# First loads in another order, a last stage on two queues and two engines, in a two-layer decoder trunk

## The chip, the cores and the metric

The kernel runs on one core of a Trainium2 chip. A core has a matrix engine (TensorE, PE in the profile), a vector engine (VectorE, DVE), an engine for functions of one argument (ScalarE, ACT), a general engine (GpSimd, POOL) and one that mostly issues transfers (SyncE, SP). Transfers between the chip's main memory and the core's own memory are issued into queues; an engine that issues one does so in its own order of instructions. The metric is the time of one execution on the device, in microseconds (us); smaller is better. "Profiled execution" is one further run that the hardware profiler recorded.

## The reference

Input is one sequence of 256 tokens with 1024 features and one conditioning vector c. The trunk has two layers; each is a half-step feed-forward block (FFN), a token mixer (stick-breaking attention in layer 0, a gated linear recurrence in layer 1), and another half-step FFN. Ahead of every block x is normalised and shifted and scaled by vectors that are made from c:

```
c_act = silu(c)
mod   = (c_act @ mod_w[layer] + mod_b[layer]).reshape(B, 3, 3, D)    # per block: shift, scale, gate
h     = rmsnorm(x, norm_g) * (1 + scale) + shift
x     = x + weight * (1 + gate) * block(h)                            # weight 0.5 for an FFN, 1 for a mixer
swiglu(h) = (silu(h @ w_g) * (h @ w_u)) @ w_down
...
out   = rmsnorm(x, final_norm_g)
```

All of it is in float32. Some 250 MB of weights are read once.

## The kernel before

x is kept transposed: 8 chunks of 128 features by 256 tokens, in one tile `xall`. Weights come as raw tiles of 1 MB, in a ring of three (`raw`). ScalarE rounds each to a high part (`wh`, L516) and VectorE makes the low part as the difference (`wl`, L519); TensorE adds three products per block of weights (high by high, high by low, low by high; L545).

The shift, scale and gate vectors are made by VectorE. `mod_tile` (L570 to L579) loads 512 KB of `modw` into a ring of three (`rawm`), and one instruction (L577) multiplies it by silu(c), which stands in all 128 partitions (`cact`), and adds up along the row. There are 144 such tiles. `mod_final` adds the bias and finishes a vector. `hook` (L1219) hands out these tiles between the weight tiles of each block.

All loads go through SP's one queue, in program order. The program is first recorded as a list of operations, and a planner (`Program.schedule`) then writes a fixed order for each engine: it simulates the list with a cost for each operation (`c_dma`, `c_act`, `c_dve`, `c_mm`) and takes the operation with the earliest due time among those that could start. So an edit of an early operation or of its cost can move instructions anywhere in the program, not only at the place of the edit. A load's cost is its bytes by 360 a ns plus 20 ns; the first loads wait for one another by `chained` with a latency of 950 ns (`LAT0`).

Between two blocks the work goes so. `down` (L663) finishes the 8 chunks of a block's output; `residual` (L686) adds each to x on VectorE; `add_square` (L603 to L614) squares it on ScalarE and adds the squares up on VectorE (`ssq`); `scaled` (L629 to L639) makes from it the next block's input without its norm (`hx`), in two parts. `rstd` (L616) lets TensorE sum the squares over partitions with a matrix of ones (L621), and ScalarE makes the reciprocal root (`rst`). TensorE meanwhile begins the next block on the input without norm (`up_first`, L734), and `norm_chunk` (L642 to L649) makes the input with norm. Modulation products and weight splits stand between all these on VectorE, in the order that the planner wrote.

The first block has no block before it. `first_loads` (L1175) loads x in four pieces of two chunks, c behind the first of them, and squares the chunks on ScalarE and, for chunks 1 and 7, on VectorE; TensorE spreads c over the partitions and ScalarE makes silu of it. The first scale and shift tiles, the first part of the parameters (`pars`, biases and norm weights) and the first weights (`gu0`) follow.

The last stage, `final` (L1157), multiplies x by `rst` on VectorE (L1162) in six pieces of 1, 1, 2, 2, 1 and 1 chunks, and SP stores each (L1164).

Of the kernel before, what the change touches and what calls it, by code (L numbers as in the profile page):

```python
# [10 lines left out]
AF = mybir.ActivationFunctionType  # L11
# [19 lines left out]
HALF = 1024  # L31
SQ = 8
NFIRST = 2
LAT0 = 950.0
SMALL = (0, 7)
HXPAD, HKPAD, ARPAD = 112, 16, 64
KICKS = (2, 3, 7, 9, 11, 15, 19)
# [321 lines left out]
    return (432.0 if passes == 4 else 114.0 * passes) * max(n, 256) / 256  # L359


def c_dma(n):
    return n * P * 4 / 360.0 + 20.0


@with_exitstack
def trunk(ctx, tc, xT, cb, par, modw, gu0, gu, wdn, qk, wv, wo, win, wri, wout, out):
# [74 lines left out]
    def fixed(name, cols, dt=F32):  # L442
        return const.tile([P, cols], dt, tag=name, name=name)
# [35 lines left out]
    def col(off, n=1):  # L479
        return pars()[:, off : off + n]  # L480
# [6 lines left out]
    fixed("pad1", ARPAD)  # L487


    def dma(dst, src, n, w, after=(), lat=None):  # L490
        return pr.op("DMA", c_dma(n), lambda: sp.dma_start(dst(), src), w=w, after=after, lat=lat)

    def A(o, i, f, n, r, w, table=None, psum=False, ptr=0, after=(), **kw):
        def fn():
            act.activation(o(), i(), f, **{k: (v() if callable(v) else v) for k, v in kw.items()})  # L495
        return pr.op("ACT", c_act(n, psum, ptr), fn, r, w, after, table)

    def V(fn, n, r, w, cost=None, ptr=0):
        return pr.op("DVE", cost or c_dve(n) + 62.0 * ptr, fn, r, w)
# [67 lines left out]
        return acc.group(part, o, w, wc, xs, xc, stop, parts)  # L567


    def mod_tile(l, s, w, t, after=(), lat=None):  # L570

        m = mraw[l, s, w]
        raw = Buf(modr)
        load_ = dma(raw, modw[l, (s * 3 + w) * KD + t], D, [raw], after, lat)

        def fn():
            dve.scalar_tensor_tensor(raw(), raw(), 1.0, cact(), ALU.mult, ALU.mult, accum_out=m()[:, t : t + 1])  # L577
        V(fn, D, [raw, cact], [raw, (m, t)])
        return load_  # L579

    def mod_final(l, s, w, t0=0, n=KD):
        m, f = mraw[l, s, w], mfin[l, s, w]
        b = OFF_MB + (l * 9 + s * 3 + w) * KD + t0
        rr = [(m, t) for t in range(t0, t0 + n)]
        ww = [(f, t) for t in range(t0, t0 + n)]
        pp = [(pars, 0)] if l == s == 0 else [pars]
        mi = lambda: m()[:, t0 : t0 + n]
        fo = lambda: f()[:, t0 : t0 + n]
        if w == 0:
            V(lambda: dve.tensor_tensor(fo(), mi(), col(b, n), ALU.add), n, rr + pp, ww)  # L590
            return
        V(lambda: dve.tensor_tensor(mi(), mi(), col(b, n), ALU.add), n, rr + pp, rr)
        if w == 1:
            g = OFF_NG + (l * 3 + s) * KD + t0
            V(lambda: dve.scalar_tensor_tensor(fo(), mi(), 1.0, col(g, n), ALU.add, ALU.mult), n, rr + pp, ww)
        else:
            wt = MAC if s != 1 else 1.0
            V(lambda: dve.tensor_scalar(fo(), mi(), 1.0, wt, ALU.add, ALU.mult), n, rr, ww)
# [172 lines left out]
    def ffn(l, s, nxt, hook):  # L771
        j = 2 * l + (s == 2)
        R, F = new_phase(2 * NF * 2, 0)
        ys = []

        def tile_out():
            ys.append((Buf(R, 2), Buf(R, 2)))
            return ys[-1]

        if j == 0:  # L780
            f0 = SQ
            accs = [Acc(f"g0_{f}") for f in range(SQ)]
            q = rstd((0, 0))

            def early(k, w):
                if k < KD:
                    last[:] = [mod_tile(0, 0, w, k, last, LAT0)]
                    if k == 0 and w == 0:
                        chained(lambda: pars()[:, :NP0], par[:, :NP0], NP0, [(pars, 0)])
                        mod_final(0, 0, 1, k, 1)  # L790
                    if k or w == 0:
                        mod_final(0, 0, w, k, 1)

            early(0, 1)
            early(0, 0)
            dma(lambda: pars()[:, NP0:], par[:, NP0:], NPAR - NP0, [(pars, 1)])
            for k in range(KD):
                norm_chunk((0, 0), k, q)
                size = HALF // 2 if k in SMALL else HALF
                done = [0]  # L800

                def chain(dst, src, n, w):
                    chained(dst, src, n, w)
                    done[0] += n
                    if done[0] % HALF == 0:
                        early(k + 1, 2 - done[0] // HALF)

                ws = load(gu0[k], CH, f"gu0_{k}", chain, size)
                for f in range(SQ):
                    for g in range(2):  # L810
                        i, c0 = divmod((f * 2 + g) * P, size)
                        group(accs[f], (g, 0), lambda b, g=g: b[:, g * T : (g + 1) * T], ws[i],
                              lambda u, c0=c0: u[:, c0 : c0 + P], hcur[0, 0][k], lambda v: v[:, :T], T, k == KD - 1)
            for f in range(SQ):
                swiglu_tile(accs[f], tile_out())
            other_copy((0, 0))
        else:
            f0 = NFIRST

            def first_out(g, gr, gc, u, ur, uc):  # L820
                sg, a = Buf(sgr), Buf(ar)
                A(sg, g, AF.Silu, T, [g, gr], [sg], table="silu", ptr=1, bias=gc)
                V(lambda: dve.scalar_tensor_tensor(a(), u(), uc(), sg(), ALU.add, ALU.mult), T, [u, ur, sg], [a], ptr=1)
                split(tile_out(), a, T)

            for (g, gr, gc), (u, ur, uc) in up_first((l, s), [load(gu[j, f], CH, f"gu_{j}_{f}") for f in range(f0)]):
                first_out(g, gr, gc, u, ur, uc)
        for f in range(f0, NF):
            hook(f)
            acc = Acc(f"g_{j}_{f}")  # L830
            up(acc, load(gu[j, f], CH, f"gu_{j}_{f}", chained if j == 0 and f == f0 else None), (l, s), f in KICKS)
            swiglu_tile(acc, tile_out())
        down(l, s, nxt, [wdn[j, :, 2 * c : 2 * c + 2, :].rearrange("p k d -> p (k d)") for c in range(NF // 2)],
             lambda k: (ys[k], slice(0, T)), 2, lambda c: hook(NF + 2 * c))
# [322 lines left out]
    def final():  # L1157
        q = rstd("end")

        def put(d0, n):  # L1160
            o = xall[:, d0 * T : (d0 + n) * T].rearrange("p (d t) -> p d t", d=n)
            V(lambda: dve.tensor_tensor(o, o, q().unsqueeze(1).to_broadcast([P, n, T]), ALU.mult), n * T,  # L1162
              x[d0 : d0 + n] + [q], x[d0 : d0 + n])
            pr.op("DMA", c_dma(n * T), lambda: sp.dma_start(out[:, d0 : d0 + n, :], o), x[d0 : d0 + n], [])  # L1164

        for d0, n in ((0, 1), (1, 1), (2, 2), (4, 2), (6, 1), (7, 1)):
            put(d0, n)


    last = []  # L1170

    def chained(dst, src, n, w):
        last[:] = [dma(dst, src, n, w, last, LAT0)]

    def first_loads():  # L1175
        c, b = Buf(modr), [Buf(banks), Buf(banks)]

        total = Buf(ssqr)

        def square(d):  # L1180
            p, q = [total if d + i == 0 else Buf(sqr if i else hpr) for i in range(2)]
            A(p, x[d], AF.Square, T, [x[d]], [p])
            if d in (0, KD - 2):
                V(lambda: dve.tensor_tensor(q(), x[d + 1](), x[d + 1](), ALU.mult), T, [x[d + 1]], [q])
            else:
                A(q, x[d + 1], AF.Square, T, [x[d + 1]], [q])

            def add(a, b):
                V(lambda: dve.tensor_tensor(a(), a(), b(), ALU.add), T, [a, b], [a])

            if d == KD - 2:
                add(p, q)
                ssq[0, 0] = (total, p)
            else:
                if d:
                    add(total, p)
                add(total, q)

        for d in range(0, KD, 2):
            o = xall[:, d * T : (d + 2) * T].rearrange("p (d t) -> p d t", d=2)  # L1200
            chained(lambda o=o: o, xT[:, d : d + 2, :], 2 * T, x[d : d + 2])
            if d == 0:
                last[:] = [pr.op("DMA", 450.0, lambda: sp.dma_start(c()[:1, :], cb), [], [c], last, lat=LAT0 - 440.0)]
                for h in range(2):
                    cs = slice(h * 512, (h + 1) * 512)
                    pr.op("PE", 4 * 427.0, lambda h=h, cs=cs: pe.matmul(b[h]()[:, :], ones[:1, :], c()[:1, cs], start=True,
                                                                        stop=True), [c], [b[h]])
                    A(lambda cs=cs: cact()[:, cs], b[h], AF.Silu, 512, [b[h]], [(cact, h)], table="silu", psum=True)
            square(d)

    first_loads()

# [92 lines left out]
```

## Time and profile before

| what | us |
|---|---|
| median of three runs | 964.43 |
| the three runs | 965.01, 964.43, 962.86 |
| the profiled execution | 971.47 |
| its span, which the rows below count from 0 | 969.8 |
| TensorE busy in the span | 950.1 |
| VectorE busy | 796.6 |
| ScalarE busy | 563.3 |
| GpSimd busy | 2.3 |

The mean granted clock of TensorE in the profiled execution was 0.996 of full speed. A row of a timeline reads: start, duration, engine, line of the kernel and operation, what is written from what is read, number of instructions taken together, and in brackets how long the engine stood idle before it and what ended that. A row of a group reads: line, engine, operation, count, then busy time and mean duration in ns, then idle time before. A row of stages reads: stretch, its length, busy time (and instructions) of TensorE, its weight loads, VectorE, ScalarE and GpSimd, the granted clock, the busy share of the transfer engines, and GB/s.

### The profile page before, as it was taken

The page shows a single profiled execution, that of the slowest core. Times are in us where ns is not written, and L with a number is a line of the kernel's source. Part 1 is how long each engine was busy: PE and PEld are TensorE (multiplying, and loading weights), DVE is VectorE, ACT ScalarE, POOL GpSimd, SP SyncE. Part 2 cuts the span into 40 slices and gives each one's busy share as a digit, 9 for nine tenths or more (in the row PEclk, how much of TensorE's full clock was granted, in tenths as well). Part 3 has the DMA queues.
Part 4 walks back from the last instruction along what each step waited for, and adds up shares of the span by engine and source line. Part 5 has one row for each costly group of instructions (what it writes and reads, how often), then busy time and mean ns, then how long its engine had stood idle before and what let it go on. Part 6 is the DMA issues. An engine that isn't in the chain of part 4 may idle for free.

```text
span 969.8 us, 19744 instructions
## 1 busy us (share of the span) xinstructions
PE 950.1 (98%) x8102; PEld 937.1 (97%) x8102; DVE 796.6 (82%) x1322; ACT 563.3 (58%) x908; POOL 2.3 (0%) x15
## 2 busy tenths in 40 slices
PE   6999999999999999999999999999999999999996
PEld 4999999999999999999989999999999999999996
DVE  7998888798998999889789999854997997555443
ACT  5475444388886854454356544443879785454343
POOL 0000000000000000000000000000000000000000
PEclk9999999999999999999999999999999999999999
DMA  8989999945766399999976999975334646555531
GB/s 315 369 308 357 323 355 353 344 190 188 252 216 207 139 362 334 338 352 363 345 255 237 339 366 355 345 276 189 116 137 168 261 142 250 199 193 192 172 116 44
DMA packets 48332, 251.25 MB, mean 259 GB/s; under 512 B 5489, under 2 KB 6129, under 8 KB 28530
## 3 DMA queue, kind: packets, MB, share of 16 engines
q1 hardware_dynamic: 48242, 249.99, 70.6%
q8 instruction: 63, 1.03, 0.4%
q14 instruction: 27, 0.22, 0.1%
HBM read 248.92 MB, written 1.05 MB: 258 GB/s over the span
## 4 chain that ended last, share of the span: by engine, by line
PE 71%; DVE 12%; DMA 10%; ACT 3%; issue 2%; SPq 1%; DVEq 0%
PE bank L545 65%; DMA rawm<-in_modw 10%; DVE wl L519 4%; DVE rawm L577 3%; PE bank L866 2%; DVE arenaf L1045 1%; PE bank L989 1%; ACT wh L516 1%; ACT arenaf L495 1%; DMA raw<-in_gu 1%; PE bank L562 1%; PE bank L942 1%; DVE x L686 1%; DVE hx L649 1%; PE bank L967 1%
## 5 line engine op out<-in xcount | busy, mean ns | idle before, releaser
L545 PE MATMUL bank<-hx,wh 128*128 128x256 f32 (+1 forms) x3236 | 564.8, 279 | 3.9 <-ACT hx L495 3.1
L545 PEld LDWEIGHTS bank<-hx,wh 128*128 128x128 f32 x3236 | 493.7, 189 | 6.6 <-ACT hx L495 3.9
L516 ACT ACTIVATE wh<-raw 128x1024 fp32r<-128x1024 f32 (+1 forms) x328 | 336.7, 1046 | 273.1 <-PE bank L545 192.6
L519 DVE TENSOR_TENSOR wl<-raw,wh 128x1024 fp32r<-128x1024 f32 (+1 forms) x328 | 388.7, 1207 | 97.2 <-ACT wh L516 96.2
L545 PE MATMUL bank<-hx,wl 128*128 128x256 f32 (+1 forms) x1618 | 449.8, 278 | 0.0
L545 PEld LDWEIGHTS bank<-hx,wl 128*128 128x128 f32 x1618 | 306.1, 189 | 0.0
L545 PE MATMUL bank<-arenar,wh 128*128 128x256 f32 x1664 | 285.0, 277 | 0.0
L545 PEld LDWEIGHTS bank<-arenar,wh 128*128 128x128 f32 x1664 | 250.8, 188 | 0.1
L545 PE MATMUL bank<-arenar,wl 128*128 128x256 f32 x832 | 229.7, 276 | 0.0
L577 DVE SCALAR_TENSOR_TENSOR rawm<-rawm,cact 128x1024 f32<-128x1024 f32 x144 | 174.8, 1220 | 31.6 <-DMA rawm<-in_modw 31.1
L545 PEld LDWEIGHTS bank<-arenar,wl 128*128 128x128 f32 x832 | 156.2, 188 | 0.0
L495 ACT ACTIVATE arenar<-a 128x256 fp32r<-128x256 f32 x88 | 35.5, 406 | 23.2 <-DVE a L764 18.9
L769 DVE TENSOR_TENSOR arenar<-a,arenar 128x256 fp32r<-128x256 f32 x88 | 36.3, 418 | 1.0 <-ACT arenar L495 1.0
L495 ACT ACTIVATE sg<-bank 128x256 f32<-128x256 f32 x82 | 30.0, 367 | 8.9 <-PE bank L545 8.8
L764 DVE TENSOR_TENSOR a<-bank,sg 128x256 f32<-128x256 f32 x82 | 34.0, 417 | 1.5 <-ACT sg L495 1.1
L495 ACT ACTIVATE hx<-hpre,mf 128x256 fp32r<-128x256 f32 x48 | 23.4, 500 | 17.3 <-DVE mf L590 12.3
L495 ACT ACTIVATE hx<-x,mf 128x256 fp32r<-128x256 f32 x40 | 18.8, 502 | 22.3 <-DVE x L686 22.3
L545 PE MATMUL bank<-hk,wh 128*128 128x256 f32 x156 | 31.0, 290 | 0.0
L686 DVE SCALAR_TENSOR_TENSOR x<-bank,mf,x 128x256 f32<-128x256 f32 x48 | 21.7, 477 | 7.8 <-PE bank L545 7.7
L545 PEld LDWEIGHTS bank<-hk,wh 128*128 128x128 f32 x156 | 24.0, 188 | 0.5
L649 DVE SCALAR_TENSOR_TENSOR hx<-hpre,mf,hx 128x256 fp32r<-128x256 f32 x48 | 22.9, 480 | 1.8 <-ACT hx L495 1.8
L866 PE MATMUL bank<-wh,hx 128*128 128x256 f32 x128 | 23.4, 281 | 0.4 <-DVE hx L649 0.4
(106 smaller groups left out, 537.7 us busy)
## 6 DMA issues: line engine op xcount, KB each, us to landing
raw<-in_gu SPq DMA_DIRECT2D x79, 1024.0 KB, 5.6
rawm<-in_modw SPq DMA_DIRECT2D x144, 512.0 KB, 6.7
raw<-in_wdn SPq DMA_DIRECT2D x44, 1024.0 KB, 6.9
raw<-in_win SPq DMA_DIRECT2D x10, 1024.0 KB, 4.8
raw<-in_qk SPq DMA_DIRECT2D x8, 1024.0 KB, 5.5
raw<-in_gu SPq DMA_DIRECT2D x14, 512.0 KB, 5.7
raw<-in_wout SPq DMA_DIRECT2D x5, 1024.0 KB, 5.3
raw<-in_wv SPq DMA_DIRECT2D x4, 1024.0 KB, 4.9
```

The lines of the kernel that those rows point to most:

```text
L495: act.activation(o(), i(), f, **{k: (v() if callable(v) else v) for k, v in kw.items()})
L516: act.activation(h()[:, :m], raw()[:, a : a + m], AF.Copy)
L519: dve.tensor_tensor(lo()[:, :m], raw()[:, a : a + m], f32(h()[:, :m]), ALU.subtract)
L545: pe.matmul(o(b()), wc(u()), xc(v()), start=start and n == 0, stop=stop and n == len(passes) - 1, skip_group_check=True)
L562: pr.op("PE", c_mm(n, 4), lambda: pe.matmul(o(b()), wc(w()), xc(x32()), start=start, stop=stop, skip_group_check=True), [w, x32] + ([] if ...
L577: dve.scalar_tensor_tensor(raw(), raw(), 1.0, cact(), ALU.mult, ALU.mult, accum_out=m()[:, t : t + 1])
L649: V(lambda: dve.scalar_tensor_tensor(lo()[:, :T], hp(), sh()[:, c], f32(hi()[:, :T]), ALU.add, ALU.subtract), T, [hp, (sh, d), hi], [lo], ...
L686: dve.scalar_tensor_tensor(x[d](), acc.b()[:, j * T : (j + 1) * T], gate()[:, d : d + 1], x[d](), ALU.mult, ALU.add)
L764: V(lambda: dve.tensor_tensor(a(), b()[:, T:], sg(), ALU.mult), T, [(b, (1, 0)), sg], [a])
L769: V(lambda: dve.tensor_tensor(y[1](), a(), f32(y[0]()), ALU.subtract), n, [a, y[0]], [y[1]])
L866: pe.matmul(o, u()[:, tb * P : (tb + 1) * P], v()[:, c0 : c0 + 256], start=start and n == 0, stop=k == KD - 1 and n == 2, skip_group_check ...
L942: pe.matmul(zb[e]()[:, BL[i]], v()[rows, kc], w()[rows, qc], start=False, stop=i == 1 and n == 2, skip_group_check=True)
```

## The change

The row of c is loaded first, then x in two pieces of four chunks. The first part of the parameters is issued from ScalarE's queue instead of SP's. The squares are split anew: ScalarE makes those of chunks 1, 2, 3, 5 and 6, VectorE those of 0, 4 and 7, and each half of x has a sum of squares of its own; TensorE adds the two. The first scale tile is multiplied in two halves of 512 columns, whose sums one further small instruction joins. The planner counts the first loads at 390 bytes a ns where it counted 360. In the last stage VectorE multiplies chunks 0, 1, 4, 5, 6 and 7 one by one and GpSimd chunks 2 and 3 in one instruction; chunks 0, 4 and 6 are stored by SP, chunk 1, the pair 2 and 3, and chunks 5 and 7 by ScalarE. The planner writes all orders anew.

```diff
-LAT0 = 950.0
+LAT0, RATE0, RATE = 950.0, 390.0, 360.0
...
-def c_dma(n):
-    return n * P * 4 / 360.0 + 20.0
+def c_dma(n, rate=RATE):
+    return n * P * 4 / rate + 20.0
...
+    def act_dma(dst, src, r, w, lat=2600.0):
+        return pr.op("ACT", 60.0, lambda: act.dma_start(dst(), src), r, w, lat=lat)
...
             def early(k, w):
                 if k < KD:
-                    last[:] = [mod_tile(0, 0, w, k, last, LAT0)]
-                    if k == 0 and w == 0:
-                        chained(lambda: pars()[:, :NP0], par[:, :NP0], NP0, [(pars, 0)])
-                        mod_final(0, 0, 1, k, 1)
-                    if k or w == 0:
-                        mod_final(0, 0, w, k, 1)
-
-            early(0, 1)
+                    last[:] = [mod_tile(0, 0, w, k, last, LAT0, RATE0)]
+                    mod_final(0, 0, w, k, 1)
+
+            def first_scale():
+                m, f, half = mraw[0, 0, 1], mfin[0, 0, 1], Buf(ap=fixed("mhalf", 8))
+                raw = Buf(modr)
+                chained(raw, modw[0, KD], D, [raw])
+                for h, o in enumerate((m, half)):
+                    cs = slice(h * 512, (h + 1) * 512)
+                    V(lambda cs=cs, o=o: dve.scalar_tensor_tensor(raw()[:, cs], raw()[:, cs], 1.0, cact()[:, cs], ALU.mult,
+                                                                  ALU.mult, accum_out=o()[:, :1]), 512,
+                      [(raw, h), (cact, h)], [(raw, h), (o, 0)])
+                bo, g = OFF_MB + KD, OFF_NG
+                V(lambda: dve.scalar_tensor_tensor(m()[:, :1], m()[:, :1], half()[:, :1], col(bo), ALU.add, ALU.add), 1,
+                  [(m, 0), (half, 0), (pars, 0)], [(m, 0)])
...
+            first_scale()
             early(0, 0)
...
     def final():
         q = rstd("end")
 
-        def put(d0, n):
+        def put(d0, n, eng, queue):
             o = xall[:, d0 * T : (d0 + n) * T].rearrange("p (d t) -> p d t", d=n)
...
-        for d0, n in ((0, 1), (1, 1), (2, 2), (4, 2), (6, 1), (7, 1)):
-            put(d0, n)
+            def scale():
+                (dve if eng == "DVE" else pool).tensor_tensor(o, o, q().unsqueeze(1).to_broadcast([P, n, T]), ALU.mult)
+            pr.op(eng, c_dve(n * T) if eng == "DVE" else 150.0 + 2.2 * n * T, scale, xs + [q], xs)
+            if queue == "SP":
+                pr.op("DMA", c_dma(n * T), lambda: sp.dma_start(out[:, d0 : d0 + n, :], o), xs, [])
+            else:
+                act_dma(lambda: out[:, d0 : d0 + n, :], o, xs, [])
+
+        for d0, n, eng, queue in ((0, 1, "DVE", "SP"), (2, 2, "POOL", "ACT"), (1, 1, "DVE", "ACT"), (4, 1, "DVE", "SP"),
+                                  (5, 1, "DVE", "ACT"), (6, 1, "DVE", "SP"), (7, 1, "DVE", "ACT")):
+            put(d0, n, eng, queue)
...
     def chained(dst, src, n, w):
-        last[:] = [dma(dst, src, n, w, last, LAT0)]
+        last[:] = [dma(dst, src, n, w, last, LAT0, RATE0)]
 
     def first_loads():
         c, b = Buf(modr), [Buf(banks), Buf(banks)]
...
+        act_dma(lambda: pars()[:, :NP0], par[:, :NP0], [], [(pars, 0)])
+        last[:] = [pr.op("DMA", 450.0, lambda: sp.dma_start(c()[:1, :], cb), [], [c], last, lat=LAT0 - 440.0)]
...
+        total = []
+        for d in range(0, KD, 4):
+            o = xall[:, d * T : (d + 4) * T].rearrange("p (d t) -> p d t", d=4)
+            chained(lambda o=o: o, xT[:, d : d + 4, :], 4 * T, x[d : d + 4])
+            t, q, u, v = Buf(ssqr), Buf(hpr), Buf(sqr), Buf(sqr)
+            for i, (z, eng) in enumerate(((t, "DVE"), (q, "ACT"), (u, "ACT"), (v, "DVE" if d else "ACT"))):
+                square(d + i, z, eng)
+                if i:
+                    add(t, z)
+            total.append(t)
+        ssq[0, 0] = tuple(total)
```

More of the change, by code (lines that the diff above doesn't have):

```diff
@@ L487, in trunk, with dma @@
     fixed("pad1", ARPAD)
-    def dma(dst, src, n, w, after=(), lat=None):
-        return pr.op("DMA", c_dma(n), lambda: sp.dma_start(dst(), src), w=w, after=after, lat=lat)
+    def dma(dst, src, n, w, after=(), lat=None, rate=RATE):
+        return pr.op("DMA", c_dma(n, rate), lambda: sp.dma_start(dst(), src), w=w, after=after, lat=lat)
+    def act_dma(dst, src, r, w, lat=2600.0):
+        return pr.op("ACT", 60.0, lambda: act.dma_start(dst(), src), r, w, lat=lat)
     def A(o, i, f, n, r, w, table=None, psum=False, ptr=0, after=(), **kw):
@@ L567, in group, with mod_tile @@
         return acc.group(part, o, w, wc, xs, xc, stop, parts)
-    def mod_tile(l, s, w, t, after=(), lat=None):
+    def mod_tile(l, s, w, t, after=(), lat=None, rate=RATE):
         m = mraw[l, s, w]
         raw = Buf(modr)
-        load_ = dma(raw, modw[l, (s * 3 + w) * KD + t], D, [raw], after, lat)
+        load_ = dma(raw, modw[l, (s * 3 + w) * KD + t], D, [raw], after, lat, rate)
         def fn():
@@ L786, in early @@
                 if k < KD:
-                    last[:] = [mod_tile(0, 0, w, k, last, LAT0)]
-                    if k == 0 and w == 0:
-                        chained(lambda: pars()[:, :NP0], par[:, :NP0], NP0, [(pars, 0)])
-                        mod_final(0, 0, 1, k, 1)
-                    if k or w == 0:
-                        mod_final(0, 0, w, k, 1)
-            early(0, 1)
+                    last[:] = [mod_tile(0, 0, w, k, last, LAT0, RATE0)]
[12 more added lines that the diff above has]
+                  [(m, 0), (half, 0), (pars, 0)], [(m, 0)])
+                V(lambda: dve.scalar_tensor_tensor(f()[:, :1], m()[:, :1], 1.0, col(g), ALU.add, ALU.mult), 1,
+                  [(m, 0), (pars, 0)], [(f, 0)])
+            first_scale()
             early(0, 0)
@@ L1158, in final @@
         q = rstd("end")
-        def put(d0, n):
+        def put(d0, n, eng, queue):
             o = xall[:, d0 * T : (d0 + n) * T].rearrange("p (d t) -> p d t", d=n)
-            V(lambda: dve.tensor_tensor(o, o, q().unsqueeze(1).to_broadcast([P, n, T]), ALU.mult), n * T,
-              x[d0 : d0 + n] + [q], x[d0 : d0 + n])
-            pr.op("DMA", c_dma(n * T), lambda: sp.dma_start(out[:, d0 : d0 + n, :], o), x[d0 : d0 + n], [])
-        for d0, n in ((0, 1), (1, 1), (2, 2), (4, 2), (6, 1), (7, 1)):
-            put(d0, n)
+            xs = x[d0 : d0 + n]
+            def scale():
[5 more added lines that the diff above has]
+                act_dma(lambda: out[:, d0 : d0 + n, :], o, xs, [])
@@ L1170, in trunk @@
+        for d0, n, eng, queue in ((0, 1, "DVE", "SP"), (2, 2, "POOL", "ACT"), (1, 1, "DVE", "ACT"), (4, 1, "DVE", "SP"),
+                                  (5, 1, "DVE", "ACT"), (6, 1, "DVE", "SP"), (7, 1, "DVE", "ACT")):
+            put(d0, n, eng, queue)
     last = []
     def chained(dst, src, n, w):
-        last[:] = [dma(dst, src, n, w, last, LAT0)]
+        last[:] = [dma(dst, src, n, w, last, LAT0, RATE0)]
     def first_loads():
         c, b = Buf(modr), [Buf(banks), Buf(banks)]
-        total = Buf(ssqr)
@@ L1180, in square @@
[L1180 to L1184, printed above, removed]
-            else:
[L1186 to L1209, printed above, removed]
+        act_dma(lambda: pars()[:, :NP0], par[:, :NP0], [], [(pars, 0)])
@@ new lines, in first_loads, with square @@
+        last[:] = [pr.op("DMA", 450.0, lambda: sp.dma_start(c()[:1, :], cb), [], [c], last, lat=LAT0 - 440.0)]
+        for h in range(2):
+            cs = slice(h * 512, (h + 1) * 512)
+            pr.op("PE", 4 * 427.0, lambda h=h, cs=cs: pe.matmul(b[h]()[:, :], ones[:1, :], c()[:1, cs], start=True, stop=True),
+                  [c], [b[h]])
+            A(lambda cs=cs: cact()[:, cs], b[h], AF.Silu, 512, [b[h]], [(cact, h)], table="silu", psum=True)
+        def square(d, q, eng):
+            if eng == "ACT":
+                A(q, x[d], AF.Square, T, [x[d]], [q])
+            else:
+                V(lambda: dve.tensor_tensor(q(), x[d](), x[d](), ALU.mult), T, [x[d]], [q])
@@ new lines, in add @@
+        def add(a, b):
+            V(lambda: dve.tensor_tensor(a(), a(), b(), ALU.add), T, [a, b], [a])
+        total = []
[8 more added lines that the diff above has]
+            total.append(t)
```

## The prediction

> **What bounds the kernel now.** I read the engine table and the chain of waits first, then the busy time by stage, then the timelines of the stages that the change touches. On the page's engine table, on the shares of its chain that ended last and on the row of the modulation products:
>
> ```profile
> PE 950.1 (98%) x8102; PEld 937.1 (97%) x8102; DVE 796.6 (82%) x1322; ACT 563.3 (58%) x908; POOL 2.3 (0%) x15
> ...
> PE 71%; DVE 12%; DMA 10%; ACT 3%; issue 2%; SPq 1%; DVEq 0%
> ...
> L577 DVE SCALAR_TENSOR_TENSOR rawm<-rawm,cact 128x1024 f32<-128x1024 f32 x144 | 174.8, 1220 | 31.6 <-DMA rawm<-in_modw 31.1
> ```
>
> TensorE is the bound on average, but 25% of the chain is VectorE, transfers and ScalarE. VectorE waits for nothing as long as for the modulation weights (31.1 of 31.6 us before L577). The stages (stretch; busy TensorE, weight loads, VectorE, ScalarE, GpSimd; granted clock; DMA share; GB/s) tell where that matters:
>
> ```profile
> 38.00:52.00 14.00, 13.64 (x115) 13.05 (x114) 13.86 (x25) 6.39 (x8) 0.00 (x0) 1.00 1.00 330
> 123.00:200.00 77.00, 77.00 (x681) 76.97 (x680) 65.91 (x106) 33.28 (x51) 0.00 (x0) 1.00 0.95 353
> 200.00:210.00 10.00, 9.16 (x74) 8.91 (x74) 9.72 (x25) 9.38 (x20) 0.00 (x0) 1.00 0.41 143
> 350.00:495.00 145.00, 145.00 (x1280) 144.96 (x1279) 126.91 (x196) 66.71 (x96) 0.00 (x0) 1.00 0.93 348
> 505.00:515.00 10.00, 8.40 (x53) 8.02 (x54) 9.86 (x20) 9.80 (x18) 0.00 (x0) 0.83 0.55 211
> 960.00:969.80 9.80, 1.92 (x10) 1.00 (x8) 3.12 (x7) 2.67 (x6) 0.00 (x0) 0.79 0.30 108
> ```
>
> From 123 to 200 and from 350 to 495 TensorE never rests: nothing gained or lost there shows. It rests at the start, at the end (1.92 busy of the last 9.80), and where one sub-layer's residual turns into the next one's input: the first FFN into attention (near 205, "T1") and layer 0 into layer 1 (near 508, "T2"). At both VectorE is nearly full.
>
> **The change, part by part.**
>
> *First loads.* The conditioning row goes ahead, x comes in two loads of 512 KB for four of 256 KB, the parameters leave SP's queue for ScalarE's. Before:
>
> ```profile
> DMA to landing us min/median/max: 3.2/4.0/6.3
> ...
> 0.80 0.39 SPq L491 DMA_DIRECT2D x<-in_xT  x1
> 1.24 0.32 SPq L1203 DMA_DIRECT2D rawm<-in_cb  x1
> 3.90 0.45 SPq L491 DMA_DIRECT2D pars<-in_par  x1
> 4.00 0.42 ACT L495 ACTIVATE ssq<-x 128x256 f32<-128x256 f32 x1 [1.92 <-DMA x<-in_xT]
> 4.13 3.75 PE L1206 MATMUL bank<-rawm,ones 1*128 1x512 f32 x4 [4.13 <-DMA rawm<-in_cb]
> 8.82 0.42 DVE L1184 TENSOR_TENSOR sq<-x 128x256 f32<-128x256 f32 x1 [0.83 <-DMA x<-in_xT]
> 9.14 0.58 ACT L495 ACTIVATE cact<-bank 128x512 f32<-128x512 f32 x1
> 10.20 1.23 DVE L577 SCALAR_TENSOR_TENSOR rawm<-rawm,cact 128x1024 f32<-128x1024 f32 x1 [0.43 <-DMA rawm<-in_modw]
> 11.35 0.08 DVE L577 DVE_READ_ACCUMULATOR rawm<-rawm,cact 128x1 f32 x1
> 13.52 0.68 DVE L519 TENSOR_TENSOR wl<-raw,wh 128x512 fp32r<-128x512 f32 x1
> ...
> 2.00:6.00 4.00, 1.87 (x3) 0.85 (x4) 2.03 (x6) 1.21 (x4) 1.00 (x6) 1.00 0.78 230
> 8.00:12.00 4.00, 2.44 (x4) 1.00 (x4) 2.65 (x5) 3.00 (x5) 0.00 (x0) 1.00 1.03 399
> ```
>
> The last x piece lands at 8.82, the first at 4.00. The bytes are the same (1.05 MB), so late is 8.8 again. Early is: the first 0.26 MB at 4.0, plus 0.44 for the row now ahead (1.24 − 0.80), plus 0.79 MB at the later 399 GB/s, 2.0: 6.4. Behind the second piece VectorE has six short operations ahead of its first product (square, four adds, square): 6 x 0.43 = 2.6. The first product starts at 9.0 to 11.4, against 10.20. That product is now two halves, each 0.68 (L519 is the 512-wide row) plus 0.08, against 1.23 plus 0.08: +0.2. The conditioning row was at 4.13 and is not what the product waited for (it waited for its weights); it gains nothing there, and the two Silu of 0.58, queued on ScalarE behind the squares, end 2.0 after the second piece (two squares of 0.42 come first), inside VectorE's 2.6. The parameters' issue costs SP 0.45 less, hidden under the loads already queued, and ScalarE some 0.45 before its table load, hidden because it waited for x until 4.00. So the start moves by −1.0 to +1.4; the stage that follows is at VectorE's limit (13.86 of 14.00 in 38 to 52), so it passes the shift on. I take the middle, +0.3: the rate of 2 to 6 us belongs to the start itself.
>
> *T1.* The planner now prices early loads differently, and its written order shifts by whole modulation tiles. Before, one product stands ahead of the last two splits and the first residuals, and one behind these; after, one more product (and 0.52 MB on SP's queue) stands ahead of the weight splits and residuals, and two instead of one inside the chain of squares.
>
> ```profile
> 191.27 1.22 DVE L577 SCALAR_TENSOR_TENSOR rawm<-rawm,cact 128x1024 f32<-128x1024 f32 x1 [2.39 <-DMA rawm<-in_modw]
> 192.42 2.35 DVE L519 TENSOR_TENSOR wl<-raw,wh 128x1024 fp32r<-128x1024 f32 x2
> 194.70 0.87 DVE L686 SCALAR_TENSOR_TENSOR x<-bank,mf,x 128x256 f32<-128x256 f32 x2
> 195.48 1.21 DVE L577 SCALAR_TENSOR_TENSOR rawm<-rawm,cact 128x1024 f32<-128x1024 f32 x1
> 196.62 0.48 DVE L639 SCALAR_TENSOR_TENSOR hx<-x,mf,hx 128x256 fp32r<-128x256 f32 x1
> 205.30 0.41 DVE L614 TENSOR_TENSOR ssq<-ssq,sq 128x256 f32<-128x256 f32 x1
> 205.76 0.70 PE L621 MATMUL bank<-ssq,ones 128*128 128x256 f32 x2 [0.84 <-DVE ssq L614]
> ...
> DVE rawm L577 <- DMA rawm<-in_modw: 10.0, 10, 2.4
> ```
>
> From 191.27 on VectorE is on the path without a pause: product, splits, residuals, squares' sums, and TensorE waits for their end (0.84). The extra product's tile ends 0.49 MB later on SP's queue than the one awaited at 191.27 (64.60 against 64.11 MB, added up over the loads that each program issues on it), at 353 GB/s 1.4: it can start at 192.66 and the chain is 1.4 late; one more product inside it is 196.62 − 195.48 = 1.14. Sum +2.5, all shown on TensorE, as it waits there already. What waits behind it on VectorE is everything of the residual; who waits is ScalarE's hx and TensorE's sum over partitions. If the tile is there in time the two terms shrink to nothing (a rival below), so the bounds are 0 and +2.5; I take +2.5, since ten waits of up to 2.4 in this stretch say that each tile here comes when the queue lets it.
>
> *T2.* The same, two tiles ahead for the same weights:
>
> ```profile
> 497.71 1.22 DVE L577 SCALAR_TENSOR_TENSOR rawm<-rawm,cact 128x1024 f32<-128x1024 f32 x1 [1.12 <-DMA rawm<-in_modw]
> 498.86 0.48 DVE L639 SCALAR_TENSOR_TENSOR hx<-x,mf,hx 128x256 fp32r<-128x256 f32 x1
> 508.20 1.18 PE L621 MATMUL bank<-ssq,ones 128*128 128x256 f32 x2 [1.47 <-DVE ssq L614]
> ```
>
> The tile now ahead of the splits ends at 147.96 MB of the queue, the one awaited at 497.71 at 148.52: at 348 GB/s it is there 1.6 earlier, at 496.1. Then product 1.15, two splits 2.35, two residuals 0.8, a product 1.15: the chain goes on at 501.6 where it did at 498.86, +2.7; one sum of squares fewer (0.41) stands behind the last split. The upper bound is +2.3. The lower is 0: the tile needs only be there by 493.4. I take the middle, +1.2. Other turns of sub-layers keep TensorE full before and have nearly the same order after: 0, hidden by TensorE's queue of matmuls.
>
> *The end.* Stores leave from two queues and GpSimd multiplies chunks 2 and 3:
>
> ```profile
> 963.07 2.63 DVE L1162 TENSOR_TENSOR x<-x,rst 128x512 f32<-128x512 f32 x6 [2.19 <-ACT rst L495]
> 963.79 3.36 SPq L1164 DMA_DIRECT2D out<-x  x6
> 966.54 0.61 SPq L1164 DMA_DIRECT2D out<-x  x1
> ...
> DMA to landing us min/median/max: 2.2/2.5/2.6
> ...
> 2.00 0.38 POOL L466 MEMSET a<- 128x256 f32 x1
> 1.35 0.29 POOL L455 TENSOR_SCALAR_AFFINE_SELECT a<-a 128x128 f32<-128x128 f32 x1
> ```
>
> SP's issues set the end: (966.54 − 963.79)/5 = 0.55 each, the last 0.84 after VectorE is done at 965.70. With four on ScalarE and three on SP the last goes out at 963.79 + 3 x 0.55 = 965.4, so −1.1. GpSimd has no row of this operation; scaled from the two shown, 512 columns are 0.8 (2 x 0.38) to 1.2 (4 x 0.29). If the two engines keep each other out, VectorE's last chunk comes 1.2 later, issued at 966.6 (+0.1); if GpSimd comes after VectorE's six chunks, it ends near 966.3, and the stores of chunks 5 and 7 queue behind its own on ScalarE: the last at 967.5, +1.0. Side by side or not: no row shows two inputs on both. I take the middle of −1.1 and +1.0, −0.1.
>
> The Trainium skill speaks here against the change (SBUF — State Buffer, section Who interferes with whom): a VectorE instruction with two inputs in SBUF and a GpSimd instruction that reads SBUF share a read port, and one blocks the other for the whole instruction. By that rule the end would be +0.1 to +1.0 and the sum up to 1.1 higher; no run so far shows it.
>
> Sum: 0.3 + 2.5 + 1.2 − 0.1 = +3.9. It stands against the profiled execution (971.47, span 969.8), which is 7.04 above the median of 964.43; by the shift alone the median becomes 968.3.
>
> **The rivals.**
> (a) Not slower: the transfers of T1 and T2 come in time when nothing is recorded (the profiled run is 7 us longer, and part may be such waits). Without its wait the awaited product at T1 starts at 191.27 − 2.39 = 188.88, the extra one at 190.1; splits start 1.2 earlier than before, and the extra product inside takes 1.1 back: 0. At T2 likewise. It decides from the extra tile's landing by 190.1. Left: 0.3 − 0.1, 964.6. Against it: the ten waits.
> (b) Faster: (a), and x lands by 6.4 (−1.0) and GpSimd runs beside VectorE (−1.1): 962.3. For it: 399 GB/s so shortly after; against it: 230 in 2 to 6.
> (c) Worse: TensorE's longer rest at T1 lowers its clock, as the 0.83 at 505 to 515 against 1.00 at 200 to 210. The ten microseconds there at 0.83 cost 8.4 x 0.17 = 1.4; with x late (+1.1) 970.8. The rule above, alone, ends at 969.4.
>
> **How the numbers follow.** The forecast, 968.3, has 4 in 10, its own range 966.4 to 970.0; (a) 2, (b) 2, (c) 2. Under 0.2% (1.9 us, what a measurement of this kernel can tell) nothing is told. Faster than 962.5: (b), 0.2; within: (a) and a little of the forecast, 0.22; slower: 0.58. The range takes in (b)'s value and most of (c): 962.1 to 971.2.
>
> **What would show it.** First product at 9.0 to 11.4; at T1 TensorE's wait for the sums of squares 3.3 for 0.84 and the sum's matmul near 208; at T2 2.7 for 1.47; the last store's issue at 965.4 to 967.5. Wrong it is if the wait at T1 stays under 1, or if the start moves by more than 1.5.

## The result, and the profile after

The changed kernel takes 980.32 us (median of four runs, 978.61 to 980.63) against 964.72 for the kernel before (962.86 to 965.24): a ratio of 1.0162, 95% interval 1.0144 to 1.0180. It is 15.6 us slower; forecast were 968.3 and a range of 962.1 to 971.2. The direction was right, the size four times too small.

The recorded execution of the changed kernel took 980.3 us, so it is an ordinary one, with a span of 978.6. Its page has these lines for engines and chain, then for VectorE's modulation products:

```profile
PE 960.4 (98%) x8102; PEld 948.4 (97%) x8102; DVE 799.1 (82%) x1325; ACT 564.4 (58%) x907; POOL 3.9 (0%) x16
...
PE 88%; DVE 6%; DMA 3%; ACT 2%; issue 1%; SPq 0%; DVEq 0%; ACTq 0%
...
L580 DVE SCALAR_TENSOR_TENSOR rawm<-rawm,cact 128x1024 f32<-128x1024 f32 x143 | 174.1, 1221 | 24.1 <-DMA rawm<-in_modw 23.4
```

Against the trace before, VectorE waits less for modulation weights (24.1 against 31.6 us), TensorE's share of the chain is up from 71% to 88%, and TensorE is busy 10 us longer with the same 8102 matmuls. But that trace was of an execution 7 us above the median. In a second trace of the kernel before (e4 below) VectorE waits 23.6 us there and TensorE is busy 946.4 us: the shorter wait is not the change's doing, and TensorE's 14 us more are nearly the whole loss. The stages of the changed kernel, columns as in the prediction:

```profile
38.00:52.00 14.00, 13.13 (x110) 12.83 (x109) 12.36 (x25) 7.12 (x8) 0.00 (x0) 1.00 0.94 355
123.00:200.00 77.00, 77.00 (x660) 76.96 (x658) 66.73 (x107) 33.84 (x51) 0.00 (x0) 1.00 0.94 351
200.00:210.00 10.00, 10.00 (x86) 9.97 (x84) 9.76 (x21) 8.47 (x17) 0.00 (x0) 1.00 0.53 185
350.00:495.00 145.00, 145.00 (x1260) 144.96 (x1260) 128.50 (x199) 67.40 (x99) 0.00 (x0) 1.00 0.94 345
505.00:515.00 10.00, 10.00 (x83) 9.95 (x83) 10.00 (x20) 8.85 (x17) 0.00 (x0) 1.00 0.39 150
```

Two things stand here. At the two turns, where the prediction put its loss, TensorE now has no pause at all. And in 123 to 200, where TensorE is full in both traces at a granted clock of 1.00, it starts 660 matmuls in the 77 us where the kernel before started 681; from 350 to 495 it is 1260 for 1280. The matmuls themselves have become slower, but only some of them. The groups by operand, kernel before and then changed kernel, show which (busy time, mean ns):

```profile
L545 PE MATMUL bank<-hx,wl 128*128 128x256 f32 (+1 forms) x1618 | 449.8, 278 | 0.0
L545 PE MATMUL bank<-arenar,wh 128*128 128x256 f32 x1664 | 285.0, 277 | 0.0
L545 PE MATMUL bank<-arenar,wl 128*128 128x256 f32 x832 | 229.7, 276 | 0.0
```

```profile
L548 PE MATMUL bank<-hx,wl 128*128 128x256 f32 (+1 forms) x1618 | 449.8, 278 | 0.0
L548 PE MATMUL bank<-arenar,wh 128*128 128x256 f32 x1664 | 297.1, 282 | 0.0
L548 PE MATMUL bank<-arenar,wl 128*128 128x256 f32 x832 | 233.7, 281 | 0.0
```

Only the matmuls whose moving operand is `arenar`, the block's intermediate result, are slower, by 5 ns each: 2496 x 5 ns = 12.5 us. (Matmuls overlap, so the sums of busy time are no path.) The program tells why these. `arenar` is allocated behind the fixed small tiles, and the change adds one of them, `mhalf`, of 32 bytes in each partition. `arenar` thereby starts at byte 161888 of a partition instead of 161856. No other tile that existed before has moved, except `arenaf` behind it.

### The profile page after: what moved, and what is told of

Its sections match the earlier page's. It is cut to its first block, busy times and chain, and to the rows that moved or that the text cites. A ratio compares the mean times of both kernels' runs of the same rounds, so it can differ in the third digit from the quotient of the medians.

```text
span 978.6 us, 19751 instructions
## 1 busy us (share of the span) xinstructions
PE 960.4 (98%) x8102; PEld 948.4 (97%) x8102; DVE 799.1 (82%) x1325; ACT 564.4 (58%) x907; POOL 3.9 (0%) x16
## 4 chain that ended last, share of the span: by engine, by line
PE 88%; DVE 6%; DMA 3%; ACT 2%; issue 1%; SPq 0%; DVEq 0%; ACTq 0%
PE bank L548 82%; DMA raw<-in_gu 3%; PE bank L880 2%; DVE wl L522 2%; DVE arenaf L1059 1%; PE bank L1003 1%; ACT arenaf L498 1%; PE bank L565 1%; DVE rawm L580 1%; ACT wh L519 1%; PE bank L956 1%; PE bank L981 1%; DVE arenaf L1056 0%; PE bank L624 0%; PE bank L983 0%
## 5 line engine op out<-in xcount | busy, mean ns | idle before, releaser
L548 PE MATMUL bank<-arenar,wh 128*128 128x256 f32 x1664 | 297.1, 282 | 0.0
L548 PEld LDWEIGHTS bank<-arenar,wh 128*128 128x128 f32 x1664 | 255.2, 188 | 0.1
L548 PE MATMUL bank<-arenar,wl 128*128 128x256 f32 x832 | 233.7, 281 | 0.0
L580 DVE SCALAR_TENSOR_TENSOR rawm<-rawm,cact 128x1024 f32<-128x1024 f32 x143 | 174.1, 1221 | 24.1 <-DMA rawm<-in_modw 23.4
```

The source lines that it names most:

```text
L548: pe.matmul(o(b()), wc(u()), xc(v()), start=start and n == 0, stop=stop and n == len(passes) - 1, skip_group_check=True)
```

## The experiments

Each run is set beside the kernel before, run on the same chip. The chips differ from one group of runs to the next, and with them the median of the kernel before (964.1 to 965.3 us), so a difference of two medians from different groups is good to about 1 us. `arenar` is moved with the length of `pad1`, an unused tile ahead of it; its columns are 4 bytes.

**The place of `arenar`: undone in the changed kernel, done alone in the kernel before.**

```diff
-HXPAD, HKPAD, ARPAD = 112, 16, 64
+HXPAD, HKPAD, ARPAD = 112, 16, 56      # e1, in the changed kernel: arenar back at 161856
+HXPAD, HKPAD, ARPAD = 112, 16, 72      # e2, in the kernel before: arenar at 161888
+HXPAD, HKPAD, ARPAD = 112, 16, 80      # e3, in the kernel before: arenar at 161920
```

> The changed kernel with one number changed: the pad behind the small tiles (pad1) is 8 columns shorter, so that the new 32-byte tile mhalf no longer pushes the block outputs (arenar) 32 bytes up in every partition: they start at byte 161856 again, as before, not at 161888. Every engine's order is that of the changed kernel. Theory A (the place of arenar costs TensorE time, as its groups bank<-arenar,wh and bank<-arenar,wl are busy 297.1 + 233.7 = 530.8 us against 285.0 + 229.7 = 514.7 before): 16 us come back, 962.5 to 967; 399 matmuls in 145 to 190 of the trace where the changed kernel has 383. Rival B (the new order of modulation tiles and loads slows the stretches where the down products run): 978 to 982, 383 matmuls.

> The kernel before with pad1 8 columns longer: arenar starts at byte 161888, where the changed kernel has it; nothing else differs, in no engine's order. Theory A: 964.7 + 16 = 978 to 982, with arenar groups near 530 us. Rival B: 963 to 966, arenar groups near 515.

> The kernel before with pad1 16 columns longer: arenar starts at byte 161920, 64 bytes up. If what costs is a start that is no multiple of 64 bytes (161856 and 161920 are, 161888 is not): 963 to 966 and arenar groups near 515 us. If it is the distance to another tile or any move from the tuned place: above 970.

Measured: e1 969.72 us (ratio 1.0057, 1.0040 to 1.0073), e2 975.49 (1.0118, 1.0104 to 1.0131), e3 979.09 (1.0154, 1.0141 to 1.0168), all against 964.21. The groups of e1, e2 and e3, in this order:

```profile
L548 PE MATMUL bank<-arenar,wh 128*128 128x256 f32 x1664 | 285.0, 277 | 0.0
L548 PE MATMUL bank<-arenar,wl 128*128 128x256 f32 x832 | 229.7, 276 | 0.0
```

```profile
L545 PE MATMUL bank<-arenar,wh 128*128 128x256 f32 x1664 | 297.1, 282 | 0.0
L545 PE MATMUL bank<-arenar,wl 128*128 128x256 f32 x832 | 233.7, 281 | 0.0
```

```profile
L545 PE MATMUL bank<-arenar,wh 128*128 128x256 f32 x1664 | 301.1, 284 | 0.0
L545 PE MATMUL bank<-arenar,wl 128*128 128x256 f32 x832 | 235.4, 283 | 0.0
```

With not one instruction moved, 32 bytes make the matmuls of the kernel before as slow as in the changed kernel, and taking them back makes those of the changed kernel as fast as before. From 145 to 190 us e1 starts 400 matmuls again where the changed kernel starts 383. That is 10.6 us (980.32 − 969.72; 10.1 by the two ratios) one way and 11.3 (975.49 − 964.21) the other. I had put 16 us on it, from the sums of busy time, which count overlapped time: too much. So e1 ends above its range, e2 below its own, and 5.5 us have another cause. The guess that a multiple of 64 bytes matters falls with e3: 64 bytes cost more than 32.

**What about its place counts.** e4 is the kernel before, unchanged. e7 and e11 move `arenar` further, or down. e8 puts 64 bytes ahead of all rings, so that weights, `hx` and `arenar` move together.

```diff
-HXPAD, HKPAD, ARPAD = 112, 16, 64
+HXPAD, HKPAD, ARPAD = 112, 16, 96      # e7: arenar at 161984
+HXPAD, HKPAD, ARPAD = 112, 16, 56      # e11: arenar at 161824
...
+    const.tile([P, 16], F32, tag="pad9", name="pad9")      # e8
     rawr, _ = ring("raw", 3, CH)
```

> The kernel before, unchanged, for a second trace and for the spread. If the TensorE waits at the two turns (near 205 and 508 us, with half the clock for 3.4 us) belong to the kernel, they are there again; if they belong to the one recorded execution, they are gone, the arenar groups are 515 us all the same, and the recorded time is near the median, 964.7. Time 963 to 966 either way.

> The kernel before with arenar 128 bytes up, at 161984. If TensorE's loss depends on the place within 128 bytes (fast at 64 past a multiple of 128, slower at 96 and at 0): 963 to 966 and arenar groups at 285.0 and 229.7 us. If the period is longer or the tuned place is single: above 970.

> The kernel before with 64 bytes put ahead of the first ring, so that weights (wh, wl), hx and arenar all move by 64 together: arenar is at 161920, where it alone cost 15 us. If what counts is how the moving operand lies to the weights: 963 to 966, arenar groups at 285.0 and 229.7. If the moving operand's own place counts: 975 or more, as hx suffers too.

> The kernel before with pad1 8 columns shorter: arenar 32 bytes down, at 161824. Modulo 512 the weights wh and wl start at 128 and arenar then at 32; before it is at 64, and it was slower at 96 (282 and 281 ns a matmul), 128 (284 and 283) and 192 (280 and 279). If the cost grows as the moving operand's place modulo 512 nears the weights' own: no cost here, groups at 277 and 276 ns, 963 to 966. If any move from the tuned place costs: above 970.

Measured: e4 965.27 us; e7 974.35 (1.0094, 1.0078 to 1.0109); e8 964.70 (0.9996, 0.9985 to 1.0006); e11 972.87 (1.0088, 1.0073 to 1.0102). The groups of e8, e7 and e11:

```profile
L546 PE MATMUL bank<-arenar,wh 128*128 128x256 f32 x1664 | 285.0, 277 | 0.0
```

```profile
L545 PE MATMUL bank<-arenar,wh 128*128 128x256 f32 x1664 | 295.7, 280 | 0.0
```

```profile
L545 PE MATMUL bank<-arenar,wh 128*128 128x256 f32 x1664 | 294.7, 280 | 0.0
```

e8 settles that it is not `arenar`'s own address: at 161920 it costs 15 us alone (e3) and nothing when the other tiles have moved as far. What counts is how it lies to them, and since these instructions read `arenar` and the weights, the weights are the likely partner; that pair was not isolated. What the rule is stays open. With `arenar` moved by −32, 0, 32, 64 and 128 bytes a matmul on `wh` took 280, 277, 282, 284 and 280 ns: a period of 128 bytes is out by e7, and my next guess (dearer as it nears the weights' place modulo 512) by e11.

e4 answers another question. Set against the same kernel, its ratio is 1.0007 (0.9994 to 1.0021), which is the measure for the small differences below. And its trace, the second of the unchanged kernel, is nearer the median (964.9 us). Here are 195 to 215 and 495 to 520, first as in the trace that the prediction used, then as in e4:

```profile
195.00:215.00 20.00, 18.75 (x155) 18.30 (x154) 19.69 (x49) 17.09 (x37) 0.00 (x0) 1.00 0.55 211
495.00:520.00 25.00, 23.14 (x173) 22.07 (x172) 22.57 (x52) 20.23 (x37) 0.00 (x0) 0.93 0.53 195
```

```profile
195.00:215.00 20.00, 20.00 (x170) 19.95 (x169) 18.93 (x46) 16.84 (x33) 0.00 (x0) 1.00 0.33 127
495.00:520.00 25.00, 24.03 (x202) 23.72 (x201) 24.13 (x51) 19.38 (x34) 0.00 (x0) 1.00 0.43 155
```

The lower clock at T2 belonged to that one execution, which was 7 us above the median: in every other trace the clock is 1.00 there. So did TensorE's wait of 0.84 us at T1. At T2 a wait of 1.0 us is left in e4, and one of 1.5 us is in e6 below; the other traces with the order of the kernel before have none. These waits come and go from one execution to the next.

**The other 5.5 us: the order at the start.** The planner's new rate turns VectorE's early order from product, split, product, split into pairs. e5 changes the rate in the kernel before and nothing else; e9 has the changed first loads at a rate that keeps products and splits in turn.

```diff
-LAT0 = 950.0
+LAT0, RATE0, RATE = 950.0, 390.0, 360.0      # e5, with RATE0 in c_dma of the first loads, no other edit
...
-LAT0, RATE0, RATE = 950.0, 390.0, 360.0
+LAT0, RATE0, RATE = 950.0, 375.0, 360.0      # e9, from the changed kernel: with ARPAD 56 and final() of before
```

> The kernel before in which the planner alone is changed: the first loads are counted at 390 bytes a ns, no load, product or store is edited, arenar stays at 161856. VectorE's early order turns from product and split in turn to products in pairs (T T h w w T T h w w), as in the changed kernel. Theory A (pairs free the rawm slots two at a time, so the loads of gu0 behind them on SP's queue leave late and ScalarE's wh waits): slower by 2 to 5 us, 966.5 to 969, with ScalarE's waits for in_gu between 14 and 70 us near 20 us, where the second trace of the kernel before has 14.4 and the changed kernel with arenar back 22.5. Rival B (the loss at the start is from the first loads themselves, two pieces of x and the parameters on another queue): 963 to 966, waits near 14.

> The changed first loads, squares and split first product, with the last stage of before, arenar back at 161856 (pad1 of 56 columns), and the planner's rate for first loads 375 instead of 390: VectorE's early order then has products and splits in turn (T h w T w T h w) instead of pairs. Theory A (the loss at the start of the changed kernel is the pairs, not its first loads): ScalarE's waits for in_gu between 14 and 70 us fall from 22.5 to 8 to 15 us, TensorE is at its matmul 675 no later than the kernel before (93.8 us in its second trace; 97.5 with the changed kernel's order): 962 to 965.5. Rival B (the first loads themselves cost): 966.5 to 969.

Measured: e5 967.54 us, ratio 1.0013 (1.0000 to 1.0026); e9 965.31 us, ratio 1.0015 (1.0003 to 1.0027). ScalarE's waits between 14 and 70 us for the first block's weights (us in total, times, longest), in e1, e5, e9 and e4:

```profile
ACT wh L519 <- DMA raw<-in_gu: 22.5, 14, 4.1
```

```profile
ACT wh L516 <- DMA raw<-in_gu: 22.8, 16, 5.1
```

```profile
ACT wh L519 <- DMA raw<-in_gu: 14.5, 11, 3.1
```

```profile
ACT wh L516 <- DMA raw<-in_gu: 14.4, 10, 2.5
```

The wait follows the order, whichever loads are in the kernel. In the three traces with pairs (e1, e5 and the changed kernel) it is 21.0 to 22.8 us, in the eleven others 5.8 to 16.6. From 24 to 54 us TensorE starts 218 matmuls in e1 and 260 in e4 (224 in e5, 232 in the changed kernel; 248 to 260 in the eleven):

```profile
24.00:54.00 30.00, 27.02 (x218) 25.42 (x217) 27.33 (x55) 13.92 (x16) 0.00 (x0) 1.00 0.91 324
```

```profile
24.00:54.00 30.00, 29.92 (x260) 29.59 (x259) 29.65 (x57) 14.22 (x17) 0.00 (x0) 1.00 0.97 362
```

Matmul 675 (counted from 0) starts at 97.1 to 98.1 us in the three traces and at 92.8 to 94.8 in the eleven. SP's issues in the changed kernel show the mechanism (start, length):

```profile
17.46 0.33 SPq L491 DMA_DIRECT2D rawm<-in_modw  x1
17.84 0.46 SPq L491 DMA_DIRECT2D raw<-in_gu  x1
24.42 0.33 SPq L491 DMA_DIRECT2D rawm<-in_modw  x1
24.85 0.38 SPq L491 DMA_DIRECT2D raw<-in_gu  x1
```

A load of modulation weights waits for a slot of `rawm`, and the weight load behind it in the queue waits with it. In pairs the slots come free two at a time, and SP issues no load from 18.3 to 24.4, when VectorE's next product is done (23.17 to 24.39); in e4 the same two pairs of loads went out at 18.75 and 22.65. By the time alone e5 is small (1.3 us by its ratio, whose interval begins at no change; 2.3 by the medians; 3.0 by the spans of the traces, 966.2 − 963.2), so its size is better read from e12 below. e9 came out as theory A had it in wait and time; its matmul 675, at 94.6 us, is 0.8 later than expected, but no later than in others of the eleven. Its ratio puts it 1.4 us (0.3 to 2.6) above the kernel before. As e4 shows 0.7 us for no change at all, a small cost of the changed loads may be there but is not shown, and a gain is not there.

**The last stage.** e6 is the kernel before with the changed last stage; e10 the same, but VectorE multiplies chunks 2 and 3 as well.

```diff
-    ... (2, 2, "POOL", "ACT"), ...      # e6, as in the change
+    ... (2, 2, "DVE", "ACT"), ...       # e10
```

> The kernel before with the changed last stage alone, arenar at 161856. Theory A (GpSimd's product holds VectorE up by 1.1 us and the stores from ScalarE's queue land in 3.1 us for 2.3): from rst to the end 1 to 1.5 us longer, 965 to 966.5. Rival B (the last stage gains from its two queues): 962.5 to 964.

> The kernel before with the changed last stage, but VectorE multiplies chunks 2 and 3 too (the planner puts them first); stores leave from the same two queues. From the start of rst to the end, 6.8 us before and 8.0 with GpSimd. Theory A (GpSimd's product costs, by holding VectorE up): 6.2 to 6.9, VectorE's products done in 2.7 us, time 963.5 to 965.5. Rival B (the store from ScalarE's queue costs, which landed in 3.1 us for 2.3): 7.4 or more.

Measured: e6 966.65 us, ratio 1.0014 (1.0000 to 1.0027); e10 965.02 us, ratio 1.0006 (0.9995 to 1.0016). By time alone neither is told from no change. From the start of `rst` to the end it is 8.0 us in e6, in e1 and in the changed kernel, 7.4 in e12 below, whose last stage is the same, and 7.2 in e10. Of the nine traces with the old last stage seven have 6.7 to 6.9, the first trace of before 7.2 and e9 7.6. The products in the changed kernel (shortest, median and longest, ns; first and last start) and ScalarE's stores there, then the products in e10:

```profile
L1179 DVE TENSOR_TENSOR x<-x,rst x6: 410/412/1487, 971.1 to 973.8; 128x256 f32<-128x256 f32 x6
L1179 POOL TENSOR_TENSOR x<-x,rst x1: 1498/1498/1498, 971.1 to 971.1; 128x512 f32<-128x512 f32 x1
L494 ACTq DMA_DIRECT2D out<-x x4: 339/398/457, 972.9 to 974.6; - x4
DMA to landing us min/median/max: 2.8/3.1/3.1
```

```profile
L1168 DVE TENSOR_TENSOR x<-x,rst x7: 416/417/691, 957.5 to 959.8; 128x256 f32<-128x256 f32 x6, 128x512 f32<-128x512 f32 x1
```

One of VectorE's products took 1487 ns instead of 412: it stood still while GpSimd's 1498 ns ran. With GpSimd the last store leaves 3.7 to 4.0 us after the start of `rst`, in e10 3.2, so GpSimd delays it by 0.5 to 0.8 us. Two queues without GpSimd send it earlier than the old last stage does (3.2 us for 3.9 to 4.0), but that is lost behind it: from the start of the last store to the end it is 4.1 us in e10 and 3.7 to 4.3 with GpSimd, and 2.8 to 2.9 in seven of the nine old traces (3.3 and 3.6 in the other two). So e10's 7.2 lies between its two expectations, and each of them names a part: GpSimd costs, and so do the stores from two queues. Why these take longer to land no run here shows.

**The whole change with both side effects undone.**

```diff
-LAT0, RATE0, RATE = 950.0, 390.0, 360.0
+LAT0, RATE0, RATE = 950.0, 375.0, 360.0
-HXPAD, HKPAD, ARPAD = 112, 16, 64
+HXPAD, HKPAD, ARPAD = 112, 16, 56
```

> The changed kernel whole, with two numbers changed: pad1 of 56 columns (arenar back at 161856) and the planner's first rate 375 for 390 (products and splits in turn at the start). Theory A (three parts that add: arenar's place some 10.6 us, products in pairs some 2.9, the last stage 1.3 and the first loads 1.4 by their own runs): 1.3 + 1.4 above the kernel before, 966 to 968, and ScalarE's waits for in_gu from 14 to 70 us below 18. Rival B (the parts do not add; what is over after arenar's place is not the pairs): 969 to 971, as with arenar back alone.

Measured: 966.56 us, ratio 1.0021 (1.0007 to 1.0036). ScalarE's wait is 14.6 us, and theory A's range holds. Taken back one after the other, the parts are 10.6 us for `arenar`'s place, 3.2 (969.72 − 966.56; 3.5 by the ratios) for the pairs and whatever else the planner's rate moves (at matmul 675 e1 is already 4.2 us behind e12), and 2.0 (0.21% of 965) left for what the change does by intention. Such steps add up to about the whole by themselves. That the parts add is better seen in the runs of one part each: the ratios of e2, e5, e6 and e9 lie 1.18, 0.13, 0.14 and 0.15% above 1, together 1.60%, where 1.62% was measured. The three small ones are each hardly clear of nothing, so how the last 2 us split between first loads and last stage stays open. No version was faster than the kernel before.

## Why the prediction was wrong

- **The step that failed is one that was left out.** "The change, part by part" costs each instruction of the split first product, but the tile `mhalf` that it adds was not costed at all, and "from 123 to 200 and from 350 to 495 TensorE never rests: nothing gained or lost there shows" took a full TensorE for one whose pace is fixed. There lay 10.6 of the 15.6 us: 32 bytes moved `arenar`, and TensorE was full before and after, but at another pace.
- **First loads, near.** The first product started at 9.50, inside 9.0 to 11.4, and the first main matmul at 13.47 instead of 14.19. (The middle of −1.0 and +1.4 is +0.2, not the +0.3 that the sum took; the start moved by −0.7.)

```profile
9.50 0.69 DVE L799 SCALAR_TENSOR_TENSOR rawm<-rawm,cact 128x512 f32<-128x512 f32 x1
13.47 1.10 PE L548 MATMUL bank<-hx,wh 128*128 128x256 f32 x2 [2.62 <-ACT hx L498]
```

The step "it passes the shift on" was wrong: the stage behind lost 3.2 us to the pairs, by way of the slots of `rawm`. The prediction read the new order at the two turns and not at the start, where it was plainest.
- **T1 (+2.5).** Wrong. "All shown on TensorE, as it waits there already" rested on a wait of one execution. The changed kernel has the order described, but the extra product waited only 0.39 us for its tile and began at 191.66, not at 192.66, though TensorE was by then some 3 us later than before; and the sum over partitions starts without a wait, where the prediction named a wait under 1 as the sign of being wrong:

```profile
191.66 1.23 DVE L580 SCALAR_TENSOR_TENSOR rawm<-rawm,cact 128x1024 f32<-128x1024 f32 x1 [0.39 <-DMA rawm<-in_modw]
209.70 0.60 PE L624 MATMUL bank<-ssq,ones 128*128 128x256 f32 x2
```

- **T2 (+1.2).** Wrong likewise; no pause in 505 to 515. The slower matmuls hide part of the chain, though. In e1, whose matmuls are as fast as before, TensorE had a pause of 0.87 at T1:

```profile
207.89 0.40 PE L548 MATMUL bank<-hx,wh 128*128 128x258 f32 x1 [0.87 <-DVE hx L642]
```

In e12 it waited 2.1 us at T1, in two waits for `hx`, and in e9, whose instructions stand in the same order up to the last stage, not at all. So a loss of the size that the prediction put on T1 can occur there, by waits that it did not name and not in each execution. For the turns rival (a) was nearer: no loss beyond what one execution differs from the next. The lower clock of rival (c) is in no other trace either: e6 waits 1.5 us at T2 at a clock of 1.00.
- **The end (−0.1).** Measured +0.8 against the trace before (8.0 us for 7.2). The sum went by when the last store leaves, and that hardly moved: 4.0 us after the start of `rst` for 3.9, as in its case of two engines that keep each other out (+0.1). What it left out is how long the last store takes: 4.0 us to the end for 3.3. GpSimd's product took 1.5 where 0.8 to 1.2 was estimated. The Trainium skill (SBUF — State Buffer, section Who interferes with whom) says that a VectorE instruction with two inputs in SBUF contends with a GpSimd instruction that reads SBUF, and that one blocks the other for the whole instruction. The 1487 ns beside 1498 agree with it.
- **The base.** The recorded execution of before was 7.04 us above the median, and I carried this over as a constant. In the changed kernel it is none: 980.3 recorded, 980.32 median.

The range failed because its cases, but for the lower clock of (c), were about when something starts, and none was about an unchanged instruction that takes longer at full clock. That the direction came out right was mostly luck: 13.8 of the 15.6 us (10.6 + 3.2) have causes that had not been named.

## What to carry to other kernels

A new tile, however small, moves every tile allocated behind it: compare the addresses of two programs as well as their orders, and where a matmul's operand has moved, put the tile last or take its bytes from a pad. Judge a stage where TensorE is full by its matmuls per microsecond, since a full engine says nothing of its pace. And take a second trace, or one near the median, before costing a wait that stands in a single place.

## What the hardware showed that I had not expected

32 bytes more in the start address of a moving operand cost 5 ns a matmul (277 to 282 ns on `wh`), at a granted clock of 1.00, and moving all tiles together by 64 bytes cost nothing. In the stages the pace shows in no column but the count. Here is 145 to 190 us before and after, 4.0% fewer matmuls in the same full time (e2, which differs from the kernel before in the 32 bytes alone, starts 383 as well):

```profile
145.00:190.00 45.00, 45.00 (x399) 45.00 (x398) 36.99 (x60) 18.51 (x26) 0.00 (x0) 1.00 0.94 345
```

```profile
145.00:190.00 45.00, 45.00 (x383) 45.00 (x382) 36.14 (x57) 18.25 (x25) 0.00 (x0) 1.00 0.92 347
```
